# Feed-forward sums in two halves of a bank, products of 512 columns, and a new order of the mixers' steps

## The chip, the cores and the metric

The kernel runs on one core of one Trainium2 chip, with the engines TensorE (PE in the profile; its weight loads are PEld), VectorE (DVE), ScalarE (ACT), GpSimd (POOL) and SyncE (SP). The metric is the device time of one execution in microseconds (us), the median of several runs.

## What is computed

A trunk of two layers over 256 tokens of width 1024. Each layer is

```
x += 1/2 * SwiGLU(RMSNorm(x))               # ffn1: (silu(h @ w1) * (h @ w3)) @ w2, inner width 2816
h  = RMSNorm(x);  proj = h @ w_in           # width 3840: A retention, B HGRN2, C RG-LRU
x += concat(A, B, C) @ w_out                # A, B: 4 heads, chunks of 64 tokens; C: width 256
x += CrossAttn(RMSNorm(x), RMSNorm(mem))    # wq, wkv, wo; 4 heads of 256, 256 memory tokens
x += 1/2 * SwiGLU(RMSNorm(x))               # ffn2
```

and a final RMSNorm follows. All is float32; the weights of both layers, some 214 MB, are read once.

## The kernel before

The residual lies feature-major in SBUF (`xT`, 8 tiles of 128 features x 256 tokens). A float32 product on TensorE is made of float32r products: each operand is split into two parts, hi (rounded to float32r) and lo (the rest), and `mm3` (lines 175 to 179) issues hi·hi, hi·lo and lo·hi into one sum. Every product has a weight load of its own, of 128 columns, also where two that follow each other have the same weights.

The weights are packed on the host in pieces of 512 rows x 256 columns, in their order of use, and SP loads one piece (0.5 MB) with each DMA into one of four buffers `w_raw`. `_split` makes the parts: ScalarE copies to `w_hi` (line 82), VectorE subtracts to `w_lo` (line 83), three buffers each. `take`, called before a piece's products, issues loads five and splits three pieces ahead, at a priority over all else.

In `gemm_w` the weights are stationary and the activations move, 256 tokens wide: for a piece, two column tiles m, four k tiles and three products each. The feed-forward's first half uses it for w1 and w3, whose sums share a PSUM bank (the halves `[:, 0]` and `[:, 1]`, one bank per m); then VectorE multiplies the bank by the norm's `R` (line 372), ScalarE takes the silu, VectorE the product (line 376), and `split` gives the parts of g. Its second half, w2, sums 22 k tiles into one half of a bank; `add_tile` adds it to `xT` (line 345), and ScalarE and VectorE make the next norm's parts `xn_hi` and `xn_lo` (lines 257, 258).

In `gemm_x` the activations are stationary and the weights move, 256 columns wide, for two token tiles: the token-major columns of w_in, the memory's values and the last w2, which ends in the final norm (`final`).

The mixers are written as a list of steps, `STEPS`: a number is a column of w_in whose 256 columns are projected there; `decayN` are VectorE's and ScalarE's factors for HGRN2's head N (rows `E` and `qe`), `headN` its scores and values on TensorE, first token tile, then second; `rope`, `lru`, `retN`, `silu`, `ret`, `hgrn` and `lrutail` are the other branches and their outputs, `keys` the memory's keys. Then follow the values, w_out and the attention. A scheduler orders each engine's instructions within the priorities; work that is independent (keys, values) is drawn forward to fill TensorE.

A norm ends in `finish`: two products of one column per token tile (line 329; float32 products are issued as two each), a root on GpSimd, and one product of 256 columns in float32 (line 337), from which ScalarE copies `R` (line 338).

Of the kernel before, what the change touches and what calls it, by code (L numbers as in the profile page):

```python
# [26 lines left out]
SPLIT_AHEAD = 3  # L27
LOAD_AHEAD = 5
RAW_BUFS = 4
SPLIT_OFF = 100000  # L30
EVAC_OFF = 400
O_AHEAD = 1
KV_OFF = 100000
PART_BUFS = 3
E_BUFS = 1
# [15 lines left out]
SILU = "silu_and_others"  # silu, tanh, sin  # L51
# [4 lines left out]
class Weights:  # L56
    """Streams the packed pieces of the weights and splits them into two float32r parts."""

    def __init__(self, tc, pool, flat, pieces):
        self.tc, self.nc, self.pool = tc, tc.nc, pool  # L60
        self.flat, self.pieces = flat, pieces
        self.raw, self.parts = {}, {}
        self.n_load = self.n_split = self.n_take = self.off = 0

    def _load(self):
        i = self.n_load
        self.n_load += 1
        n = self.pieces[i].nk * CW
        t = self.pool.tile([P, 4 * CW], F32, name="w_raw", tag="w_raw", bufs=RAW_BUFS)
        self.nc.sync.dma_start(  # L70
            out=t[:, 0:n], in_=self.flat[self.off:self.off + P * n].rearrange("(p c) -> p c", p=P))
        self.off += P * n
        self.raw[i] = t.rearrange("p (k c) -> p k c", k=4)

    def _split(self):
        nc, i = self.nc, self.n_split
        self.n_split += 1
        nk = self.pieces[i].nk
        t = self.raw.pop(i)
        hi = self.pool.tile([P, 4, CW], F32R, name="w_hi", tag="w_hi", bufs=PART_BUFS)  # L80
        lo = self.pool.tile([P, 4, CW], F32R, name="w_lo", tag="w_lo", bufs=PART_BUFS)
        nc.scalar.copy(hi[:, 0:nk, :], t[:, 0:nk, :])  # L82
        nc.vector.tensor_tensor(  # L83
            out=lo[:, 0:nk, :], in0=t[:, 0:nk, :], in1=hi[:, 0:nk, :].bitcast(F32), op=ALU.subtract
        )
        self.parts[i] = (hi, lo)

    def take(self, key):
        i = self.n_take
        self.n_take += 1  # L90
        assert self.pieces[i].key == key, (self.pieces[i], key)
        with self.tc.high_priority(offset=SPLIT_OFF):
            while self.n_load < min(i + LOAD_AHEAD, len(self.pieces)):
                self._load()
            while self.n_split < min(i + SPLIT_AHEAD, len(self.pieces)):
                self._split()
        return (*self.parts.pop(i), self.pieces[i].nk)
# [5 lines left out]
IN_COLS = [1536, 1792, 2048, 2304] + [int(x) for x in STEPS if x.isdigit()]  # L103


# (column piece, first row tile) of xattn_wo: the first heads' rows of some columns fill the wait for the last heads
O_ORDER = [(c, 0) for c in range(O_AHEAD)] + [(c, 4) for c in range(O_AHEAD)]
O_ORDER += [(c, k0) for c in range(O_AHEAD, 4) for k0 in (0, 4)]

Piece = namedtuple("Piece", "key name l k0 nk c0")  # L110


def weight_pieces():
    """[nk * 128, 256] pieces of the weights in the order in which they are used"""
    out = []

    def gemm(key, name, l, nk, cs):
        for c in cs:
            for k0 in range(0, nk, 4):
                out.append(Piece(key, name, l, k0, min(4, nk - k0), c))  # L120

    for l in range(DEPTH):
        for f in ("ffn1", "ffn2"):
            if f == "ffn2":
                gemm("in", "w_in", l, KD, IN_COLS)
                gemm("kv", "xattn_wkv", l, KD, range(0, 2 * D, CW))
                gemm("out", "w_out", l, KD, range(0, D, CW))
                gemm("q", "xattn_wq", l, KD, range(0, D, CW))
                out += [Piece("o", "xattn_wo", l, k0, 4, c * CW) for c, k0 in O_ORDER]
            for c in range(0, FF, CW):  # L130
                gemm("w1", f + "_w1", l, KD, [c])
                gemm("w3", f + "_w3", l, KD, [c])
            gemm("w2", f + "_w2", l, KF, range(0, D, CW))
    # the first column's pieces in halves, for an early start
    return [out[0]._replace(nk=2, k0=k0) for k0 in range(0, KD, 2)] + out[2:]
# [9 lines left out]
def trunk(ctx: ExitStack, tc: tile.TileContext, a: dict, out: bass.AP, stop=None, dbg=None):  # L145
# [9 lines left out]
    class Bank:  # L155
        """A PSUM bank in which several sums may be open: only the first product clears the written bits"""
# [18 lines left out]
        def mm3(self, acc, lhs, rhs, begin, stop):  # L175
            (lh, ll), (rh, rl) = lhs, rhs
            self.mm(acc, lh, rh, begin, False)
            self.mm(acc, lh, rl, False, False)
            self.mm(acc, ll, rh, False, stop)

    class Act:
        """Activations that need a table: each table is loaded once for a run of them, in the order of the program"""
# [14 lines left out]
        def hold(self, i):  # L197
            """the next table waits for this instruction too"""
# [14 lines left out]
    W = Weights(tc, wp, a["weights"], weight_pieces())  # L213
# [37 lines left out]
    def split(hi, lo, src, scale=None):  # L251
        """hi + lo == src (* a column) with both parts in float32r"""
# [9 lines left out]
    def gemm_w(key, nk, x, accs):  # L262
        """acc += w[:, m]^T x for two column tiles m; accs = (bank, acc), x = (hi, lo) of [P, nk, S]"""
        xh, xl = x
        k0 = 0
        while k0 < nk:
            wh, wl, n = W.take(key)
            for m, (bank, acc) in enumerate(accs):
                for k in range(n):
                    sl = slice(m * P, (m + 1) * P)  # L270
                    bank.mm3(acc, (wh[:, k, sl], wl[:, k, sl]), (xh[:, k0 + k, :], xl[:, k0 + k, :]),
                             k0 + k == 0, k0 + k == nk - 1)
            k0 += n
            yield

    def gemm_x(key, nk, x, accs, begin=True):
        """accs[t] = (bank, acc), acc += x[:, t]^T w for two token tiles t"""
        xh, xl = x
        k0 = 0
        while k0 < nk:  # L280
            wh, wl, n = W.take(key)
            for t, (bank, acc) in enumerate(accs):
                for k in range(n):
                    sl = slice(t * P, (t + 1) * P)
                    bank.mm3(acc, (xh[:, k0 + k, sl], xl[:, k0 + k, sl]), (wh[:, k, :], wl[:, k, :]),
                             begin and k0 + k == 0, k0 + k == nk - 1)
            k0 += n
            yield
# [5 lines left out]
    class Norm:  # L294
        """RMSNorm of the residual: x * g goes out in two float32r parts, the 1 / rms is applied after the product"""

        def __init__(self, l, name, mem=False):
            self.gains = col(l, name)
            if not mem:
                self.hi = keep.tile([P, KD, S], F32R, name="xn_hi", tag="xn_hi", bufs=1)  # L300
                self.lo = keep.tile([P, KD, S], F32R, name="xn_lo", tag="xn_lo", bufs=1)
            self.ssq = small.tile([P, S], F32, name="ssq", tag="ssq", bufs=2)

        def parts(self, j, xj):
            split(self.hi[:, j, :], self.lo[:, j, :], xj, self.gains[:, j:j + 1])
# [777 lines left out]
```

## Time and profile before

| | us |
|---|---|
| median of 3 runs (lowest, highest) | 1275.28 (1275.21, 1276.19) |
| span of the profiled execution | 1272.7 |
| TensorE products, weight loads busy | 1256.4, 1249.8 |
| VectorE, ScalarE, GpSimd busy | 877.4, 682.3, 42.6 |

The profiled execution's own time is its span, 1272.7 us from the first to the last instruction; the median of the runs lies 2.6 us above it. A product's row lasts some 280 ns, since the rows of products overlap; how far the products stand apart is read from the chain of waits, which counts for each product the time until the next. The stretches: 6 to 204 us the first feed-forward (its second half from 140), to 387 the mixers with w_out, to 447 the attention, to 637 the second feed-forward; then the same for the second layer, with the last w2 from 1201 to 1265.

### The profile page before, as it was taken

To read this page: it belongs to the slowest core of one execution; us is meant where nothing else is said; L and a number is where in the kernel's file an instruction comes from. 1 tells how busy PE (TensorE), PEld (TensorE's weight loads), DVE (VectorE), ACT (ScalarE), POOL (GpSimd) and SP (SyncE) were. 2 spreads that over 40 slices of the span, in tenths; PEclk is the share of its full clock that TensorE was granted. 3 is DMA by queue.
4 is the path that set the end of the run, shared out by engine and by line. 5 is a ranking of instruction groups with operands and counts; after the bars stand their busy time and mean duration, and the time that the engine had idled before them with its cause. 6 is when DMAs were issued, how large, how long until landed. Compare 5 with 4: busy or idle time off the path is not lost.

```text
span 1272.7 us, 26847 instructions
## 1 busy us (share of the span) xinstructions
PE 1256.4 (99%) x11134; PEld 1249.8 (98%) x11134; DVE 877.4 (69%) x1456; ACT 682.3 (54%) x1149; POOL 42.6 (3%) x68
## 2 busy tenths in 40 slices
PE   7999999999999999999999999999999999999997
PEld 7999999999999999999999999999999999999997
DVE  7886656988776676665586665578877767666653
ACT  4554445656765654444464444465577656444543
POOL 5000000000100000000000000000001000000000
PEclk9999999999999999999999999999999999999999
DMA  8756566555465465665566665654545645666563
GB/s 269 211 175 184 174 185 190 157 149 150 117 182 165 115 184 183 183 182 182 183 209 202 181 184 179 187 177 154 159 121 149 183 133 165 183 183 182 168 181 100
DMA packets 61946, 219.64 MB, mean 173 GB/s; under 512 B 6912, under 2 KB 7168, under 8 KB 61568
## 3 DMA queue, kind: packets, MB, share of 16 engines
q1 hardware_dynamic: 60768, 213.55, 56.2%
q0 software_dynamic: 768, 3.86, 0.8%
q8 instruction: 87, 1.43, 0.5%
q10 hardware_dynamic: 288, 0.52, 0.1%
q14 instruction: 35, 0.29, 0.1%
HBM read 216.85 MB, written 1.05 MB: 171 GB/s over the span
## 4 chain that ended last, share of the span: by engine, by line
PE 83%; issue 15%; DVE 1%; DMA 0%; ACT 0%; POOLq 0%; POOL 0%; SPq 0%; ACTq 0%
PE mm L171 75%; PE aux L171 2%; PE aux L663 1%; PE mm L169 1%; PE aux L661 0%; PE aux L169 0%; DVE xn_lo L258 0%; PE aux L656 0%; PE aux L800 0%; PE aux L731 0%; PE aux L788 0%; DMA xT<-in_x_t_dram 0%; PE aux L337 0%; PE aux L901 0%; DVE w_lo L83 0%
## 5 line engine op out<-in xcount | busy, mean ns | idle before, releaser
L83 DVE TENSOR_TENSOR w_lo<-w_raw,w_hi 128x1024 fp32r<-128x1024 f32 (+1 forms) x414 | 498.9, 1206 | 281.3 <-ACT w_hi L82 278.6
L82 ACT CAST w_hi<-w_raw 128x1024 fp32r<-128x1024 f32 (+1 forms) x414 | 425.5, 1029 | 491.8 <-PE mm L171 371.3
L171 PE MATMUL mm<-xn_hi,w_lo 128*128 128x256 f32 x1728 | 487.6, 285 | 2.1 <-DVE w_lo L83 2.1
L171 PE MATMUL mm<-xn_lo,w_hi 128*128 128x256 f32 x1728 | 488.0, 284 | 0.0
L171 PE MATMUL mm<-xn_hi,w_hi 128*128 128x256 f32 x1620 | 457.8, 284 | 6.2 <-ACT w_hi L82 6.2
L171 PEld LDWEIGHTS mm<-xn_hi,w_lo 128*128 128x128 f32 x1728 | 330.4, 192 | 3.4 <-DVE w_lo L83 3.0
L171 PEld LDWEIGHTS mm<-xn_lo,w_hi 128*128 128x128 f32 x1728 | 331.6, 192 | 0.1
L171 PEld LDWEIGHTS mm<-xn_hi,w_hi 128*128 128x128 f32 x1620 | 311.1, 192 | 6.3 <-ACT w_hi L82 6.2
L171 PE MATMUL mm<-g_hi,w_hi 128*128 128x256 f32 x528 | 147.1, 280 | 0.0
L171 PE MATMUL mm<-g_lo,w_hi 128*128 128x256 f32 x528 | 146.1, 278 | 0.0
L171 PE MATMUL mm<-g_hi,w_lo 128*128 128x256 f32 x528 | 145.2, 281 | 0.0
L171 PEld LDWEIGHTS mm<-g_lo,w_hi 128*128 128x128 f32 x528 | 99.3, 188 | 0.0
L171 PEld LDWEIGHTS mm<-g_hi,w_hi 128*128 128x128 f32 x528 | 99.3, 188 | 0.0
L171 PEld LDWEIGHTS mm<-g_hi,w_lo 128*128 128x128 f32 x528 | 97.9, 188 | 0.0
L171 PE MATMUL mm<-w_hi,xn_lo 128*128 128x256 f32 x288 | 81.8, 284 | 0.0
L171 PE MATMUL mm<-w_lo,xn_hi 128*128 128x256 f32 x288 | 81.8, 284 | 0.0
L171 PE MATMUL mm<-w_hi,xn_hi 128*128 128x256 f32 x270 | 76.4, 285 | 0.0
L372 DVE TENSOR_TENSOR f_t<-mm,R 128x512 f32<-128x512 f32 x88 | 60.1, 687 | 3.6 <-ACT R L338 1.4
L171 PEld LDWEIGHTS mm<-w_hi,xn_lo 128*128 128x128 f32 x288 | 55.2, 192 | 0.1
L171 PEld LDWEIGHTS mm<-w_lo,xn_hi 128*128 128x128 f32 x288 | 55.2, 192 | 0.1
L171 PEld LDWEIGHTS mm<-w_hi,xn_hi 128*128 128x128 f32 x270 | 51.5, 192 | 0.0
L171 PE MATMUL mm<-w_lo,g_hi 128*128 128x256 f32 x176 | 49.3, 281 | 0.0
(269 smaller groups left out, 1955.7 us busy)
## 6 DMA issues: line engine op xcount, KB each, us to landing
w_raw<-in_weights_dram SPq DMA_DIRECT2D x394, 512.0 KB, 3.7
w_raw<-in_weights_dram SPq DMA_DIRECT2D x20, 256.0 KB, 2.7
m_t<-in_mem_t_dram POOLq DMA_DIRECT2D x2, 1024.0 KB, 7.9
xT<-in_x_t_dram SPq DMA_DIRECT2D x4, 256.0 KB, 4.9
cst<-in_c_cst_dram POOLq DMA_DIRECT2D x1, 696.0 KB, 6.4
gw<-in_gates_w_dram POOLq DMA_DIRECT2D x2, 256.0 KB, 8.5
fg<-in_final_norm_g_dram POOLq DMA_DIRECT2D x1, 512.0 KB, 5.9
out_dram<-y SPq DMA_DIRECT2D x2, 256.0 KB, 2.6
```

Source lines behind the costliest of these rows:

```text
L82: nc.scalar.copy(hi[:, 0:nk, :], t[:, 0:nk, :])
L83: nc.vector.tensor_tensor(out=lo[:, 0:nk, :], in0=t[:, 0:nk, :], in1=hi[:, 0:nk, :].bitcast(F32), op=ALU.subtract)
L169: nc.tensor.matmul(acc, lhsT, rhs, start=False, stop=stop, skip_group_check=True)
L171: i = nc.tensor.matmul(acc, lhsT, rhs, start=begin, stop=stop, skip_group_check=True)
L372: nc.vector.tensor_tensor(out=t, in0=uv[m].ap, in1=nrm.R[:, None, :].to_broadcast([P, 2, S]), op=ALU.mult)
L663: nc.tensor.matmul(sb[bs, i, :], ke[:, 1 + i, cb], qe[:, 1 + i, cb], start=True, stop=True, skip_group_check=True)
```

## The change

Hi and lo parts of an activation become one tile (`x[:, k, 0]` and `x[:, k, 1]`, side by side). Where the weights are stationary in a feed-forward, `mm_w` moves both through `w_hi` in one product of 512 columns, into both halves of a bank, and hi through `w_lo` in one of 256 into the second half; the two halves are added afterwards: in the first half by a ScalarE copy and a VectorE addition, before the multiplication by `R`, in w2 by a second addition in `add_tile`. w1 and w3 now have two banks each. w_in's feature-major columns, keys, w_out, wq and wo stay as three products of 256 (`mm3n`).

Where the activations are stationary, two column pieces that lie side by side are moved as 512 columns (`beside`), in the columns 0, 512, 1024 and 2560 of w_in, the values and the last w2; the order within `mm3` is new. Raw weights come in units of two pieces, in two buffers of 1 MB. The mixers' steps have a new order, both token tiles of a head are scored before their values, retention's heads are interleaved, and w_out opens four banks and starts with the k tiles 4 to 7.

```diff
-SPLIT_AHEAD = 3
-LOAD_AHEAD = 5
-RAW_BUFS = 4
+RAW_BUFS = 2
+SPLIT_AHEAD = PART_BUFS
@@ Weights._split
+        if unit.beside:
+            hi, lo = (t.rearrange("p (h k c) -> p h k c", h=2, k=2)[:, :, 0:nk, :] for t in (hi, lo))
+            t = self.raw[u].rearrange("p h (k c) -> p h k c", k=4)[:, :, at:at + nk, :]
+        nc.scalar.copy(hi, t)
+        nc.vector.tensor_tensor(out=lo, in0=t, in1=hi.bitcast(F32), op=ALU.subtract)
@@
-STEPS = ("2560 decay0 2816 head0 decay1 3328 3584 head1 decay2 0 256 head2 decay3 512 768 rope 1024 lru head3 ret0 ret1 "
-         "1280 3072 ret2 ret3 silu ret hgrn lrutail keys").split()
+STEPS = ("2560 decay0 3328 head0 decay1 3584 3072 head1 decay2 lru 0 head2 decay3 512 head3 "
+         "rope 1024 silu hgrn ret lrutail retout keys").split()
+W_COLS, X_COLS = (3328, 3584), (0, 512, 1024, 2560)
@@ Bank
         def mm3(self, acc, lhs, rhs, begin, stop):
             (lh, ll), (rh, rl) = lhs, rhs
             self.mm(acc, lh, rh, begin, False)
-            self.mm(acc, lh, rl, False, False)
-            self.mm(acc, ll, rh, False, stop)
+            self.mm(acc, ll, rh, False, False)
+            self.mm(acc, lh, rl, False, stop)
+
+        def mm_w(self, wh, wl, x, begin, stop):
+            self.mm(self.ap, wh, x, begin, stop)
+            self.mm(self.ap[:, 1, :], wl, x[:, 0, :], False, stop)
@@
+    def gemm_w(key, nk, x, banks):
+        k0 = 0
+        while k0 < nk:
+            wh, wl, n = W.take(key)
+            for m, bank in enumerate(banks):
+                for k in range(n):
+                    sl = slice(m * P, (m + 1) * P)
+                    bank.mm_w(wh[:, k, sl], wl[:, k, sl], x[:, k0 + k], k0 + k == 0, k0 + k == nk - 1)
+            k0 += n
+            yield
+
+    def gemm_x(key, nk, x, banks):
+        k0 = 0
+        while k0 < nk:
+            wh, wl, n = W.take(key)
+            for t, bank in enumerate(banks):
+                for k in range(n):
+                    sl = slice(t * P, (t + 1) * P)
+                    bank.mm3(bank.ap, (x[:, k0 + k, 0, sl], x[:, k0 + k, 1, sl]), (wh[:, :, k, :], wl[:, :, k, :]),
+                             k0 + k == 0, k0 + k == nk - 1)
+            k0 += n
+            yield
@@
-    def add_tile(j, acc, scale, nxt):
-        nc.vector.scalar_tensor_tensor(out=xT[:, j, :], in0=acc, scalar=scale, in1=xT[:, j, :],
-                                       op0=ALU.mult, op1=ALU.add)
+    def add_tile(j, halves, scale, nxt):
+        for h in halves:
+            nc.vector.scalar_tensor_tensor(out=xT[:, j, :], in0=h, scalar=scale, in1=xT[:, j, :],
+                                           op0=ALU.mult, op1=ALU.add)
@@ ffn
-                uv = [mm_bank(2) for _ in range(2)]
+                t = [fp.tile([P, 2, S], F32, name="f_t", bufs=3) for _ in range(2)]
                 for u, key in enumerate(("w1", "w3")):
-                    run(gemm_w(key, KD, nrm.x, [(b, b[:, u, :]) for b in uv]))
+                    banks = [mm_bank(2) for _ in range(2)]
+                    run(gemm_w(key, KD, nrm.x, banks))
+                    for m in range(2):
+                        p = fp.tile([P, S], F32, name="f_p", bufs=3)
+                        nc.scalar.copy(p, banks[m][:, 1, :])
+                        nc.vector.tensor_tensor(out=t[m][:, u, :], in0=banks[m][:, 0, :], in1=p, op=ALU.add)
@@ final
-        for c in range(4):
+        for c in range(2):
             banks = [mm_bank(2) for _ in range(2)]
-            run(gemm_x("w2", KF, g, [(b, b[:, 0, :]) for b in banks]))
-            cs = slice(c * CW, (c + 1) * CW)
+            run(gemm_x("w2", KF, g, banks))
+            cs = slice(c * 512, (c + 1) * 512)
@@ mixer
         def hgrn_head(h):
-            hgrn(h, 0)
-            hgrn(h, 1)
+            scs = [hgrn_scores(h, t) for t in range(2)]
+            ss = [hgrn_mask(scs[t], t) for t in range(2)]
+            for t in range(2):
+                hgrn_values(h, t, *ss[t])
```

On TensorE, within a column pair of the feed-forward's first half, one k tile before (a row is line, operation, tile <- moving, stationary operand, partitions x columns of the result; numbers tell buffers apart):

```order
L171 MATMUL mm_492<-xn_hi_113,w_hi_402 128x256
L171 MATMUL mm_492<-xn_lo_114,w_hi_402 128x256
L171 MATMUL mm_492<-xn_hi_113,w_lo_403 128x256
L171 MATMUL mm_492<-xn_hi_113,w_hi_402 128x256
L171 MATMUL mm_492<-xn_lo_114,w_hi_402 128x256
L171 MATMUL mm_492<-xn_hi_113,w_lo_403 128x256
```

and now, where the first bank's last products meet the second bank's first:

```order
L206 MATMUL mm_447<-xn_110,w_hi_389 128x512
L206 MATMUL mm_447<-xn_110,w_lo_390 128x256
L206 MATMUL mm_448<-xn_110,w_hi_369 128x512
L206 MATMUL mm_448<-xn_110,w_lo_370 128x256
L206 MATMUL mm_448<-xn_110,w_hi_369 128x512
```

Two products stand where three stood, one of them twice as wide.

On VectorE, a column pair of the feed-forward's first half before (`f_t` is the bank times R, `f_s` the silu's product, `g_lo` the lo part of g):

```order
L83 TENSOR_TENSOR w_lo_1112<-w_raw_1027,w_hi_1111 128x1024
L376 TENSOR_TENSOR f_s_1066<-f_s_1066,f_t_1064 128x256
L83 TENSOR_TENSOR w_lo_1142<-w_raw_1079,w_hi_1141 128x1024
L255 TENSOR_TENSOR g_lo_186<-f_s_1059,g_hi_185 128x256
L255 TENSOR_TENSOR g_lo_186<-f_s_1066,g_hi_185 128x256
L83 TENSOR_TENSOR w_lo_1172<-w_raw_1109,w_hi_1171 128x1024
L372 TENSOR_TENSOR f_t_1199<-mm_1077,R_167 128x512
L372 TENSOR_TENSOR f_t_1206<-mm_1078,R_167 128x512
```

and now (`f_p` is ScalarE's copy of a bank's second half; the rows of line 425 are the additions):

```order
L98 TENSOR_TENSOR w_lo_1273<-w_raw_1198,w_hi_1272 128x1024
L425 TENSOR_TENSOR f_t_1194<-mm_1247,f_p_1292 128x256
L427 TENSOR_TENSOR f_t_1194<-f_t_1194,R_168 128x512
L98 TENSOR_TENSOR w_lo_1324<-w_raw_1249,w_hi_1323 128x1024
L425 TENSOR_TENSOR f_t_1195<-mm_1248,f_p_1295 128x256
L431 TENSOR_TENSOR f_s_1299<-f_s_1299,f_t_1194 128x256
L427 TENSOR_TENSOR f_t_1195<-f_t_1195,R_168 128x512
L98 TENSOR_TENSOR w_lo_1344<-w_raw_1249,w_hi_1343 128x1024
L301 TENSOR_TENSOR g_180<-f_s_1299,g_180 128x256
```

Up to three operations now stand between two splits, where one or two stood.

On TensorE in the first layer's mixers, around the first score product of HGRN2's fourth head (`half` and its number; `mem` are products of the keys, `hi,hs` the values of a head) before:

```order
L171 MATMUL mm<-mem_l,w_hi 128x256
L171 MATMUL mm<-mem_h,w_lo 128x256
L169 MATMUL mm<-mem_h,w_hi 128x256
L656 MATMUL aux<-half_2_109 128x128
L171 MATMUL mm<-mem_l,w_hi 128x256
```

and now:

```order
L206 MATMUL mm<-w_hi,xn 128x512 x4
L206 MATMUL aux<-hi,hs 128x96
L720 MATMUL aux<-half_2_106 128x128
L206 MATMUL mm<-mem_n,w_hi 128x256 x2
L206 MATMUL aux<-hi,hs 128x96
L720 MATMUL aux<-half_3_108 128x128
L206 MATMUL mm<-w_lo,xn 128x512
L206 MATMUL mm<-w_hi,xn 128x512 x2
```

The head, which stood among the keys, behind w_in's last token-major columns, now stands amid products of w_in (`w_hi,xn`), with both token tiles together.

## Rows read from the trace of the kernel before

**Rows 1.** The page: span; busy us (share) x instructions of each engine.
```profile
span 1272.7 us, 26847 instructions
PE 1256.4 (99%) x11134; PEld 1249.8 (98%) x11134; DVE 877.4 (69%) x1456; ACT 682.3 (54%) x1149; POOL 42.6 (3%) x68
```
**Rows 2.** Waits: engine, line <- waited for: total us, times, longest.
```profile
DVE w_lo L83 <- ACT w_hi L82: 278.6, 271, 2.6
...
PE mm L171 <- ACT w_hi L82: 6.2, 1, 6.2
...
PE mm L171 <- DVE w_lo L83: 2.1, 3, 1.0
```
**Rows 3.** Chain of waits in order of time: start us, us, what, products.
```profile
31.20 9.96 PE mm L171 x83
...
135.74 67.83 PE mm L171 x575
```
**Rows 4.** Chain of waits, 205 to 214 us: a norm's end.
```profile
208.85 0.34 PE aux L329 x4
...
213.25 0.43 PE aux L337 x2
```
**Rows 5.** Timeline of the loads, 212.8 to 213.8 us: start us, us, what.
```profile
212.97 0.31 PEld L337 LDWEIGHTS aux<-r_diag,mean 128*128 128x128 f32 x2
213.30 0.19 PEld L171 LDWEIGHTS mm<-xn_hi,w_lo 128*128 128x128 f32 x1
213.52 0.19 PEld L171 LDWEIGHTS mm<-xn_hi,w_hi 128*128 128x128 f32 x1
```
**Rows 6.** Groups of products: out<-in, shapes xcount | busy us, mean ns | idle before.
```profile
L171 PE MATMUL mm<-xn_lo,w_hi 128*128 128x256 f32 x1728 | 488.0, 284 | 0.0
...
L171 PE MATMUL mm<-g_lo,w_hi 128*128 128x256 f32 x528 | 146.1, 278 | 0.0
...
L171 PE MATMUL mm<-w_hi,xn_lo 128*128 128x256 f32 x288 | 81.8, 284 | 0.0
...
L171 PE MATMUL mm<-w_lo,g_hi 128*128 128x256 f32 x176 | 49.3, 281 | 0.0
...
L171 PE MATMUL mm<-w_hi,mem_l 128*128 128x256 f32 x128 | 36.6, 286 | 0.0
```
**Rows 7.** Groups of VectorE and ScalarE, same columns.
```profile
L83 DVE TENSOR_TENSOR w_lo<-w_raw,w_hi 128x1024 fp32r<-128x1024 f32 x394 | 483.2, 1227 | 263.1 <-ACT w_hi L82 260.4
...
L372 DVE TENSOR_TENSOR f_t<-mm,R 128x512 f32<-128x512 f32 x88 | 60.1, 687 | 3.6 <-ACT R L338 1.4 <-PE mm L171 0.5
...
L376 DVE TENSOR_TENSOR f_s<-f_s,f_t 128x256 f32<-128x256 f32 x88 | 33.8, 419 | 0.1
...
L345 DVE SCALAR_TENSOR_TENSOR xT<-mm,xT 128x256 f32<-128x256 f32 x56 | 23.0, 420 | 19.3 <-PE mm L171 19.2
...
L338 ACT COPY R<-aux 128x256 f32<-128x256 f32 x8 | 3.0, 371 | 6.7 <-PE aux L337 6.7
```
**Rows 8.** Stretches: us, then busy (x) of PE, PEld, DVE, ACT, POOL; clock, DMA, GB/s.
```profile
6.00:143.70 137.70, 135.42 (x1102) 134.30 (x1103) 104.65 (x163) 72.80 (x119) 16.82 (x19) 1.00 0.68 206
...
460.00:580.20 120.20, 120.20 (x1003) 120.15 (x1002) 79.45 (x106) 57.81 (x87) 0.00 (x0) 1.00 0.61 181
...
648.00:770.00 122.00, 122.00 (x1019) 121.95 (x1018) 85.70 (x123) 61.28 (x95) 0.00 (x0) 1.00 0.64 193
```
**Rows 9.** Stretches of the first mixers, same columns.
```profile
204.00:310.00 106.00, 106.00 (x1135) 104.88 (x1134) 89.34 (x204) 62.05 (x111) 3.66 (x8) 1.00 0.54 160
...
220.00:240.00 20.00, 20.00 (x211) 19.83 (x210) 18.81 (x47) 14.83 (x24) 0.56 (x1) 1.00 0.53 157
240.00:260.00 20.00, 20.00 (x212) 19.84 (x211) 18.49 (x47) 9.16 (x19) 0.76 (x2) 1.00 0.53 154
```
**Rows 10.** The page: DMA issues, xcount, KB each, us to landing.
```profile
w_raw<-in_weights_dram SPq DMA_DIRECT2D x394, 512.0 KB, 3.7
```

More of the change, by code (lines that the diff above doesn't have):

```diff
@@ L77, in _split @@
         self.n_split += 1
[L78 to L85, printed above, removed]
+        u, unit, at, nk = self.steps[i]
+        while self.n_load < len(self.pieces) and self.pieces[self.n_load][0] <= u:
+            self._load()
+        hi = self.pool.tile([P, 4 * CW], F32R, name="w_hi", tag="w_hi", bufs=PART_BUFS)
+        lo = self.pool.tile([P, 4 * CW], F32R, name="w_lo", tag="w_lo", bufs=PART_BUFS)
+        if unit.beside:
+            hi, lo = (t.rearrange("p (h k c) -> p h k c", h=2, k=2)[:, :, 0:nk, :] for t in (hi, lo))
+            t = self.raw[u].rearrange("p h (k c) -> p h k c", k=4)[:, :, at:at + nk, :]
+        else:
+            hi, lo = (t.rearrange("p (k c) -> p k c", k=4)[:, 0:nk, :] for t in (hi, lo))
+            t = self.raw[u].rearrange("p h (k c) -> p h k c", k=4)[:, at, 0:nk, :]
+        nc.scalar.copy(hi, t)
+        nc.vector.tensor_tensor(out=lo, in0=t, in1=hi.bitcast(F32), op=ALU.subtract)
         self.parts[i] = (hi, lo)
@@ L326, in finish @@
             pr = aux_bank()
-            self.R = small.tile([P, S], F32, name="R", tag="R", bufs=2) if R is None else R
             for t in range(2):
@@ L331, in finish @@
             rsqrt_col(self.rc, pr[:, 0:2], 2)
+            self.R = small.tile([P, S], F32, name="R", tag="R", bufs=2) if R is None else R
             dg = small.tile([P, 2, P], F32, name="r_diag", tag="r_diag", bufs=1)
@@ L380, in ffn @@
             run(setup or ())
-            if not last:
-                run(residual("w2", KF, (gh, gl), 0.5, nxt))
-            else:
-                final((gh, gl), fp)
+            if last:
+                return final(g, fp)
+            for c in range(0, KD, 2):
+                banks = [mm_bank(2) for _ in range(2)]
+                run(gemm_w("w2", KF, g, banks))
+                for m in range(2):
+                    add_tile(c + m, [banks[m][:, u, :] for u in range(2)], 0.5, nxt)
+            nxt.finish()
     def final(g, fp):
@@ L564, in mixer @@
         for j in (0, 2):
-            run(w_pair(hq, j))
+            w_pair(hq, j)
             v = hq[:, j:j + 2, :]
@@ L858, in mixer @@
                 x_cols(int(step))
-        v_mem = [values(h) for h in range(NH)]
-        run(residual("out", KD, (mh, ml), 1.0, nxt))
+        v_mem = values() + values()
+        for c in range(0, KD, 4):
+            banks = [mm_bank(2) for _ in range(4)]
+            for k0 in (4, 0):
+                for i in range(0, 4, 2):
+                    wh, wl, n = W.take("out")
+                    for m in range(2):
+                        for k in range(n):
+                            sl, bank = slice(m * P, (m + 1) * P), banks[i + m]
+                            bank.mm3n(bank[:, 0, :], (wh[:, k, sl], wl[:, k, sl]),
+                                      (mix[:, k0 + k, 0, :], mix[:, k0 + k, 1, :]), k0 + k == 4, k0 + k == 3)
+            for m in range(4):
+                add_tile(c + m, [banks[m][:, 0, :]], 1.0, nxt)
+        nxt.finish()
         return k_mem, v_mem
```

276 lines of the change are left out of this document (148 added, 128 removed).

## The prediction

> **What bounds the kernel now.** I read the page's table of busy times first [rows 1]: TensorE is busy for 1256.4 of 1272.7 us, its weight loads for 1249.8, VectorE for 877.4 and ScalarE for 682.3. A busy TensorE says little by itself, since its products overlap, so I then asked whom it waited for: by the table of waits, 8.3 us in all, for two parts of weights at the start [rows 2]. Nothing feeds TensorE too late; the time of the kernel is the sum of its products' spacings, and a change is worth what it takes off that sum.
>
> The spacing is in the chain of waits, where products that follow each other without a wait are merged. In the feed-forward's first half 83 products of 256 columns take 9.96 us, 120.0 ns each; in its second half 575 take 67.83 us, 118.0 ns each [rows 3]. What sets these 120 ns? Two pairs of unlike products tell it [rows 4]. Four products of one column each, every one behind its own load of 128 columns of weights, take 0.34 us, and the step from a load to the next is about 113 ns (the first of the four is already loaded: 0.34 / 3). So a load costs some 113 ns even where the product is nothing. And the two products of line 337, in float32 and 256 columns wide, stand 215 ns apart (0.43 / 2), although one of them, too, has its load between. There the product's own stream is the longer, and the load vanishes beneath it. The timeline of the loads shows the same [rows 5]: the two loads of line 337 are 0.12 us apart (0.31 less one load's 0.19), each starts when the product before it starts, then comes one after 0.33 and the next after 0.22 us, the length of the long stream. So every spacing is the longer of two: the load of the next weights, 118 to 120 ns beside a running product, and the product's own stream. A product of 256 columns is too short to cover the load that follows it.
>
> **The change, part by part.** (1) *Feed-forward with the weights stationary.* Three products of 256 columns (hi·hi, hi·lo, lo·hi) become one of 512 and one of 256. The 512 columns are not in the trace. Lower bound: 215 ns, the pair of line 337, if a float32r column takes half the time of a float32 column there. Upper bound: 240 ns, twice the 120 of today, if the stream and not the load makes the 120. I take 218, near the lower: the rows show a load of 120 gone wholly beneath a long stream, but beside float32r streams loads are 5 to 7 ns longer than the 113 of the one-column products, and part of such friction may come to lie on the stream. The 256 that follows still pays for a load, 120 (118 in the second half). First half: 4 feed-forwards x 11 column pairs x 2 matrices x 8 x 2 = 1408 triples (the other 320 of the 1728 in [rows 6] belong to other projections, which stay as three). 3 x 120 - (218 + 120) = 22 ns, 1408 x 22 = 31.0 us. Second half, three feed-forwards: the 528 triples of [rows 6], 354 - (218 + 118) = 18 ns, 9.5 us.
>
> (2) *Token-major products of 512 columns.* Two products of 256 become one of 512, all three kinds. Of the 288 x 3 with xn stationary, the four column pairs of w_in make 768; the memory's values make 128 x 3 = 384; the last product 176 x 3 = 528 [rows 6]. 576 pairs x (240 - 218) = 12.7 us, 264 pairs x (236 - 218) = 4.8 us. Sum of (1) and (2): 58.0 us.
>
> The skill speaks against this sum in one place. The Trainium skill ("TensorE: Matmul & The Clock Gate", section Back-to-back issue gap) gives the gap of a lone stream as its columns over the clock and 2.5 ns, so 109 ns for 256 columns and 216 for 512, by which 2776 products fewer would be worth 2776 x 2.5 = 7 us, as an estimate. The trace does not agree, since 256 columns stand 118 to 120 ns apart here and one column 113; I give it no chance of its own. In Part 3 of the same page of the Trainium skill (packing small matmuls, The mechanism) a load overlaps a running product only in other row groups; by that, a load would come on top of every 512 columns. The trace contradicts it with the 215 ns of line 337, which hold a stream and a load.
>
> (3) *What the other engines get.* Each column pair of the first half now sums in two halves of a bank: 4 copies on ScalarE out of PSUM (0.37 each, the row of R) and 4 additions on VectorE (0.42, the row of xT) are added, 44 per feed-forward; the multiplication by R stays at 0.69, its operand now in SBUF [rows 7]. In the first feed-forward VectorE has 104.7 us of work in 137.7 us [rows 8]; with 44 x 0.42 = 18.5 it has 123.1, while the stretch shrinks by 352 x 22 ns = 7.7 to 130.0: 95%. In the second it is 79.5 + 18.5 = 98.0 of 112.5, 87%; in the third 85.7 + 18.5 = 104.2 of 114.3, 91%. ScalarE in the second: 57.8 + 16.3 of 112.5, 66%. The cover is three split steps ahead, some 2 x 2.7 us of TensorE's work between the moment when a buffer comes free and the moment when it must be full, and by the order at most three operations (1.5 us) stand between two w_lo. So I charge 3 us for the first feed-forward and 1 for the other three (bounds 0 and 10). Behind a w_lo that is late stands TensorE itself, and nothing else.
>
> (4) *Small ends.* The first product now wants the lo part of xn as well, one more operation of VectorE (0.5 us), and the first 12 us are bound by loading and splitting, so their saving of 0.7 us is not had: 1.2 us. At the very end each addition, square and gain is 512 wide instead of 256, 0.27 us longer each on the path (0.69 against 0.42): 0.8 us. The second addition per tile in the second half adds 0.42 us to the tail of three feed-forwards; the next stage's products on the six earlier tiles cover it: nothing (1.3 us without the cover).
>
> (5) *The mixers' order.* The products that are moved cost the same. What can be lost is cover: the fourth head's scores now stand ahead of the last w_in column instead of behind it and rope, so VectorE's four decays must be done earlier, while TensorE's w_in work is shorter. VectorE is the engine that is close: 89.3 of 106.0 us over the first mixers and 18.5 to 18.8 of 20 in the stretches of the decays [rows 9]; its work there stays, and TensorE's work in the same stretch shrinks by 192 x 22 ns = 4.2 us. I charge 2 us a layer, 4 (bounds: nothing, as now, where TensorE waits for no head; and 12 us, if the stretch becomes VectorE's). The raw weights' buffers, now two of 1 MB instead of four of half, leave a load a whole unit of time (5.4 us) for the 3.7 us that it takes by the page's table of issues [rows 10]: nothing.
>
> Sum: -58.0 + 4.0 + 1.2 + 0.8 + 4.0 = -48.0. The profiled execution's span of 1272.7 us stands 2.6 under the median of the runs (1275.28), which lies around the span and stays; 1275.3 - 48.0 = **1227 us**.
>
> **The rivals.**
> *A cost per product.* The 120 ns could be 107 of stream (half of line 337's 215) and 13 that every product pays, load or not. Then 512 columns cost 226, and the change saves 13.3 ns on 1408 + 576 and 11.3 on 528 + 264: 35.3 us; with the 10 us of (3) to (5), 1250. For it: the spacing is nearly constant. Against: 215 ns for line 337, which leaves at most 2 ns over twice 107.
> *VectorE sets the pace of the first halves.* A column pair has 4 w_lo (1.23), 4 additions, 2 x 0.69 and 4 x 0.42: 9.7 us, against 11.5 of TensorE now (96 x 0.120) and 10.8 after (32 x 0.338). If 0.47 us per w_lo of its wait for w_hi (278.6 us in all now, [rows 2]) can't be filled with other work, the first halves gain nothing: 1275.3 - 27.0 + 6 = 1254. For it: a strict order on the engine. Against: that wait is one of an engine that is ahead.
> *The mixers lose their cover*: 12 us a layer instead of 2, 1247. For it, the 18.8 of 20 us; against, TensorE waits for no head now, though VectorE is as full in those stretches [rows 2, 9].
> *The other side: the stream sets the 120.* If TensorE can't take in a float32r column faster than 120 / 256 ns, 512 columns cost 240, no product gets cheaper, and (3) to (5) remain: 1285. It decides from 235 ns per 512 columns (218 + 48.0 / 2.776). For it: the spacing of 256 columns is never far below 113 to 120. Against: the 113 of the one-column products, which have no stream.
>
> **How the numbers follow.** Forecast 0.64; a cost per product 0.14; VectorE 0.09; the mixers 0.05; the stream 0.08. A measurement of this kernel can tell about 0.2% (2.6 us) from no change. The forecast's own range is 1209 (215 ns, no new stalls) to 1240. The first three rivals end under 1272 nearly always: faster 0.89, within 0.2% 0.03, slower 0.08. The range reaches to the cost per product and to VectorE's case and leaves out the stream: 1208 to 1258.
>
> **What would show it.** In the profile after: runs of 512-column products about 218 ns apart and pairs of 512 and 256 about 338; busy weight loads well under the span, since there are 2776 fewer; w_lo's waits for w_hi shrunk; TensorE's waits under 15 us, most of them in the first feed-forward for w_lo. 226 or 240 ns there make it one of two rivals; gaps of TensorE behind w_lo in the first halves, or behind hs and E in the mixers, the other two. It is wrong if the sum of spacings has fallen and the span has not.

## The result, and the profile after

The changed kernel takes 1252.72 us (median of four runs, 1251.94 to 1253.19) against 1275.39 (1275.21 to 1276.19): ratio 0.982, interval 0.9806 to 0.9834. It is faster by 22.7 us, inside the range, but less than half of the 48.0 that I forecast; the time is that of the rival "a cost per product" (1250).

The head of the page, as in [rows 1]:

```profile
span 1250.1 us, 21651 instructions
...
PE 1230.2 (98%) x8358; PEld 1102.1 (88%) x8358; DVE 938.3 (75%) x1645; ACT 733.9 (59%) x1303; POOL 43.4 (3%) x68
```

TensorE is busy to nearly the same share (98 against 99%) with 2776 products fewer, and its loads have fallen below the span by 148 us. It waits 11.4 us for others, 3 more than before; in the table of waits, which answers to [rows 2] (total us, times, longest):

```profile
PE mm L206 <- DVE xn L304: 7.1, 1, 7.1
PE mm L206 <- DVE w_lo L98: 3.4, 6, 1.1
PE mm L206 <- ACT o L300: 0.9, 2, 0.4
```

So the time is still the sum of the products' spacings. The chain of waits merges the feed-forward's products now as it did in [rows 3] (start us, us, what, products):

```profile
30.73 25.50 PE mm L206 x145
```

175.9 ns a product, every other one 512 columns wide: 352 a pair, where I forecast 338 and three products took 360. How the pair splits is in the timeline of TensorE in the second feed-forward, where the starts (first column, us) count and the durations overlap:

```profile
499.67 0.40 PE L206 MATMUL mm<-xn,w_hi 128*128 128x512 f32 x1
499.90 0.28 PE L206 MATMUL mm<-xn,w_lo 128*128 128x256 f32 x1
500.02 0.40 PE L206 MATMUL mm<-xn,w_hi 128*128 128x512 f32 x1
500.25 0.28 PE L206 MATMUL mm<-xn,w_lo 128*128 128x256 f32 x1
500.37 0.40 PE L206 MATMUL mm<-xn,w_hi 128*128 128x512 f32 x1
```

Some 230 ns behind each wide product, 120 behind each narrow one. The stretches of the changed kernel, with the columns of [rows 8] (the first feed-forward's first half; the second's; its second half, with g; the third's first half; then the two that answer to [rows 9]):

```profile
7.00:137.00 130.00, 127.98 (x714) 110.24 (x715) 114.04 (x200) 82.47 (x156) 15.57 (x19) 1.00 0.57 209
460.00:560.00 100.00, 100.00 (x568) 86.72 (x567) 78.56 (x125) 59.04 (x108) 0.00 (x0) 1.00 0.51 190
570.00:627.00 57.00, 57.00 (x329) 50.11 (x328) 34.09 (x49) 26.83 (x38) 0.00 (x0) 1.00 0.53 189
655.00:752.00 97.00, 96.75 (x557) 84.56 (x558) 79.86 (x129) 57.82 (x106) 0.00 (x0) 1.00 0.54 196
...
204.00:310.00 106.00, 104.91 (x1030) 95.25 (x1030) 90.11 (x206) 64.96 (x110) 3.47 (x8) 1.00 0.42 153
222.00:242.00 20.00, 20.00 (x180) 17.77 (x179) 17.89 (x43) 12.32 (x16) 0.00 (x0) 1.00 0.52 188
```

The clock is granted in full in all of them, and in the second to fourth TensorE is busy all but without a break while VectorE has 18 to 40% of its time left. With xn a pair takes 2 x 100 / 568 = 352 ns, with g 2 x 57 / 329 = 347. The additions cost VectorE and ScalarE what I had taken from [rows 7]; in the changed kernel's groups, same columns:

```profile
L424 ACT COPY f_p<-mm 128x256 f32<-128x256 f32 x176 | 64.2, 366 | 37.0 <-PE mm L206 35.3
L425 DVE TENSOR_TENSOR f_t<-mm,f_p 128x256 f32<-128x256 f32 x176 | 73.0, 417 | 0.1
```

### The profile page after: what moved, and what is told of

The parts are those of the page before. It is cut to its first block, busy times and chain, and to the rows that moved or that the text cites. A ratio compares the mean times of both kernels' runs of the same rounds, so it can differ in the third digit from the quotient of the medians.

```text
span 1250.1 us, 21651 instructions
## 1 busy us (share of the span) xinstructions
PE 1230.2 (98%) x8358; PEld 1102.1 (88%) x8358; DVE 938.3 (75%) x1645; ACT 733.9 (59%) x1303; POOL 43.4 (3%) x68
## 4 chain that ended last, share of the span: by engine, by line
PE 81%; issue 15%; DVE 3%; ACT 1%; DMA 0%; POOLq 0%; POOL 0%; SPq 0%; DVEq 0%; ACTq 0%
PE mm L206 74%; PE aux L206 2%; PE aux L727 1%; DVE w_lo L98 1%; PE aux L725 0%; ACT w_hi L97 0%; DMA xT<-in_x_t_dram 0%; DVE xn L304 0%; PE aux L204 0%; PE aux L720 0%; PE aux L877 0%; PE aux L806 0%; PE aux L998 0%; PE aux L863 0%; PE aux L399 0%
## 5 line engine op out<-in xcount | busy, mean ns | idle before, releaser
L206 PE MATMUL mm<-xn,w_hi 128*128 128x512 f32 (+1 forms) x2028 | 608.4, 362 | 7.1 <-DVE xn L304 7.1
L206 PE MATMUL mm<-xn,w_lo 128*128 128x256 f32 x1728 | 480.2, 282 | 2.3 <-DVE w_lo L98 2.3
L206 PEld LDWEIGHTS mm<-xn,w_hi 128*128 128x128 f32 x2028 | 360.4, 189 | 66.2 <-ACT w_hi L97 7.1
L206 PEld LDWEIGHTS mm<-xn,w_lo 128*128 128x128 f32 x1728 | 327.5, 190 | 8.7 <-DVE w_lo L98 5.3
L206 PE MATMUL mm<-g,w_hi 128*128 128x512 f32 x528 | 181.7, 392 | 0.0
L206 PE MATMUL mm<-g,w_lo 128*128 128x256 f32 x528 | 143.1, 281 | 0.0
L206 PEld LDWEIGHTS mm<-g,w_hi 128*128 128x128 f32 x528 | 96.8, 188 | 19.5
L206 PEld LDWEIGHTS mm<-g,w_lo 128*128 128x128 f32 x528 | 99.4, 188 | 2.6
L206 PE MATMUL mm<-w_hi,xn 128*128 128x512 f32 (+1 forms) x318 | 89.1, 374 | 0.0
L424 ACT COPY f_p<-mm 128x256 f32<-128x256 f32 x176 | 64.2, 366 | 37.0 <-PE mm L206 35.3
L425 DVE TENSOR_TENSOR f_t<-mm,f_p 128x256 f32<-128x256 f32 x176 | 73.0, 417 | 0.1
L404 DVE SCALAR_TENSOR_TENSOR xT<-mm,xT 128x256 f32<-128x256 f32 x80 | 32.5, 419 | 22.6 <-PE mm L206 22.6
```

Of the source, the lines that this page charges most:

```text
L206: i = nc.tensor.matmul(acc, lhsT, rhs, start=begin, stop=stop, skip_group_check=True)
L404: nc.vector.scalar_tensor_tensor(out=xT[:, j, :], in0=h, scalar=scale, in1=xT[:, j, :], op0=ALU.mult, op1=ALU.add)
L424: nc.scalar.copy(p, banks[m][:, 1, :])
L425: nc.vector.tensor_tensor(out=t[m][:, u, :], in0=banks[m][:, 0, :], in1=p, op=ALU.add)
```

## The experiments

**1. Products alone.** A kernel of nothing but products, 32 of a kind behind each other in one bank, eight loads in turn, then other places, other types, fewer stationary columns, and stretches beside VectorE, ScalarE and DMAs. In short:

```
for n in (512, 448, 384, 320, 256, 192, 128, ...):
    segment([(big[:, X0:X0 + n], big[:, (i % 8) * 128:(i % 8) * 128 + 128]) for i in range(32)])
...
```

> Products alone, 32 of a kind behind each other, with no other engine at work but in the last four stretches; the kernel's own computation is left out. In the changed kernel 512 float32r columns stand 226 to 241 ns apart where I had counted 218. Theory A, a cost per product that does not shrink with the width: (columns / 2.4 GHz) + 13 ns as long as a load of 113 ns is the shorter, so 512 -> 226, 448 -> 200, 384 -> 173, 320 -> 147, 256 -> 113 to 120, and 113 from 192 columns down; a stationary operand of 64 columns changes 512 by 0 to 7 ns. Theory B, a stream slower than one column per cycle: 512 / 448 / 384 / 320 / 256 in proportion, 240 / 210 / 180 / 150 / 120 or 226 / 198 / 170 / 141 / 113. Theory C, other engines take away reads: alone 512 -> 215 and 256 -> 113, beside VectorE's, ScalarE's or the DMAs' work 226 to 240 and 120. Theory D, addresses: the pitch of one width differs by 7 to 20 ns with the place of the moving operand.

Its chain of waits; a name gives the columns (w) and, where they are not 128, the stationary columns (m); bf is bfloat16, f float32 (each of its 32 products is issued as two, so 64 are counted):

```profile
38.90 7.25 PE x512w L208 x32
46.15 6.49 PE x448w L208 x32
52.64 5.57 PE x384w L208 x32
58.21 4.69 PE x320w L208 x32
62.90 3.84 PE x256w L208 x32
66.73 3.55 PE x192w L208 x32
70.28 3.55 PE x128w L208 x32
...
94.78 7.36 PE x512m64w L208 x32
...
113.27 3.63 PE x256m64w L208 x32
...
286.07 6.92 PE x512bf L208 x32
292.99 3.49 PE x256bf L208 x32
296.49 13.81 PE x256f L208 x64
```

Divided by the count: 227, 203, 174, 147 and 120 ns for 512 to 256 columns, that is the columns at 2.4 GHz (the clock is granted in full there) and 13 to 16 ns, whatever the width; 111 for 192 columns and for 128, a floor that I take for the load. That is theory A. Theory B falls, since 512 and 256 columns are not in proportion. The extra belongs to float32r: bfloat16 takes 216 and 109, and the two halves of a float32 product of 256 columns 216 each.

The stationary operand has a part in it, though. With 64 stationary columns instead of 128, 256 columns took 113 ns instead of 120, and 512 took 230 instead of 227. Every product here had a load of its own, so the runs do not tell what a product would pay without one.

The Trainium skill ("TensorE: Matmul & The Clock Gate", section Back-to-back issue gap) gives for the gap of an isolated product at the full clock its columns over 2.4 GHz and 2.5 ns; the bfloat16 rows agree with it, and no row in float32r does.

Theory C falls too; stretches of this kernel with TensorE alone, beside VectorE, and beside VectorE and ScalarE:

```profile
318.00:329.00 11.00, 11.00 (x63) 9.71 (x64) 0.91 (x7) 0.00 (x0) 0.00 (x0) 1.00 0.00 0
330.00:341.00 11.00, 11.00 (x64) 9.73 (x64) 10.21 (x14) 0.00 (x0) 0.00 (x0) 1.00 0.01 1
342.00:353.00 11.00, 11.00 (x64) 9.60 (x62) 10.79 (x14) 9.70 (x10) 0.00 (x0) 1.00 0.00 0
```

As many products in 11 us, whether the others rest or work. Beside DMAs, with their engines 86% busy, 256 columns took the same 120 ns, and 512 took 227 as soon as the clock was granted in full (427 before that, at half the clock). Of theory D there was a trace: with the moving operand 64 bytes further 512 columns took 233 and 256 took 118.

**2. Three products of 256 again in the feed-forwards**, without the copies and additions of the halves, all else as changed:

```
-                    bank.mm_w(wh[:, k, sl], wl[:, k, sl], x[:, k0 + k], ...)
+                    bank.mm3n(acc, (wh[:, k, sl], wl[:, k, sl]), (x[:, k0 + k, 0, :], x[:, k0 + k, 1, :]), ...)
```

> The changed kernel with the feed-forwards' products as three of 256 columns again, in both halves (the additions and copies of the halves go too); token-major products and the mixers' order stay as changed. From the traces' spacings (a triple 360 against 351 ns, 1408 times, and 354 against 348.4, 528 times) I expect 12.7 + 3.0 = 16 us more than the changed kernel, 1268. The prediction's size of 22 and 18 ns would make it 40 us more, 1293. If the additions on VectorE cost what I charged (6 us), 10 us more, 1262.

1267.69 us (1267.47 to 1268.60), ratio to before 0.9943 (0.9926 to 0.9959). The feed-forwards' part of the change brings 15.0 us of the 22.7. By their spacings the products alone bring 17.1 (the table below), so the copies, the additions and the waits that they make cost some 2 us at most. The 7.7 that are left belong to all the rest together, the token-major products (7.5 by their spacings) and the new order.

**3. The heads in an order close to the old one.**

```
-STEPS = ("2560 decay0 3328 head0 decay1 3584 3072 head1 decay2 lru 0 head2 decay3 512 head3 "
-         "rope 1024 silu hgrn ret lrutail retout keys").split()
+STEPS = ("2560 decay0 3072 head0 decay1 3328 3584 head1 decay2 0 head2 decay3 512 "
+         "rope 1024 lru head3 ret silu hgrn lrutail retout keys").split()
```

> The changed kernel with the mixers' steps in an order close to the old one: the fourth head behind rope, the last w_in column and the LRU's gates. From the stages' lengths the mixers gained 0.9 and 2.6 us where their products' spacings fell by 3.0 each, so some 2.5 us were lost in both layers. If the new order is what loses them, this kernel is 2.5 us faster, 1250; if the wider products lose them whatever the order, it is within 1 us of the changed kernel, 1252 to 1253; if the new order hides more than it loses, it is slower, 1255.

1250.52 us (1250.18 to 1251.44), ratio 0.9808 (0.9793 to 0.9822): 2.2 us faster than the changed kernel, about what a measurement can tell, and what the stages' lengths said. TensorE's waits for w_lo fall from 3.4 to 1.3 us. The new order costs some 2 us where I charged 4.

**4. Where the operands lie.** Products alone at other places within 512 bytes (s: the moving operand shifted by so many bytes), and 512 and 256 in turn (pair):

```
segment([(big[:, X0 + d:X0 + d + n], big[:, (i % 8) * 128:(i % 8) * 128 + 128]) for i in range(32)])
```

> Products alone again, 32 of a kind; the kernel's own computation is left out. With moving and stationary operand at the same place within 512 bytes, 512 columns took 226.7 ns and 256 took 120.0, but 512 and 256 in turn 352.9 for both, 6 more than their sum; with the moving operand 64 bytes further 233.3 and 117.8. Theory: the relative place within 512 bytes sets which few ns come on top, so a scan gives 226 to 234, 113 to 120 and 346 to 353 for the pair, with shifts of 32 bytes at 233 / 117 / 347 as g shows in the changed kernel, the same for a shift of the stationary operand the other way, and no change when both are shifted. Rival: the extra belongs to the change of width, and no shift moves the pair by more than 2 ns. In groups of four wide and four narrow products: 4 x 226.7 + 4 x 120 + one or two changes, 346.7 to 349 a pair.

Its chain of waits:

```profile
39.16 7.25 PE x512s0b L208 x32
46.42 3.83 PE x256s0b L208 x32
50.25 5.65 PE xpairs0b L208 x32
...
100.72 5.55 PE xpairs32b L208 x32
...
240.85 7.46 PE x512s448b L208 x32
248.32 3.63 PE x256s448b L208 x32
...
408.85 5.62 PE xgroup4g L208 x32
```

The place does move the spacing: 256 columns from 120 to 113 ns at 448 bytes, while 512 columns go the other way, 227 to 233; a pair 353 at one place and 347 at 32 bytes. It is not the place alone: at 64 bytes 512 columns took 229 here (7.33 us for the 32) and 233 in experiment 1 (7.47), behind other products. Both operands shifted alike changed nothing (5.65 us for the pairs, 3.83 for 256 columns). At no place does a pair come near 338. I first took the groups of four for 342 ns a pair, from a mean that counted fewer wide than narrow products; the row says 5.62 / 16 = 351.

**5. xn 32 bytes further.**

```
+                x = keep.tile([P, KD * 2 * S + 128], F32R, name="xn", tag="xn", bufs=1)
+                self.x = x[:, 8:8 + KD * 2 * S].rearrange("p (k u s) -> p k u s", k=KD, u=2)
```

> The changed kernel with xn 32 bytes further within its 512, nothing else. In the changed kernel a pair of 512 and 256 takes 353.3 ns with xn (which lies as the weights do within 512 bytes) and 346.7 with g (32 bytes further). If the place is the reason: 1408 x 6.7 = 9.4 us less in the first halves, 960 products of 256 at 117 to 118 instead of 120, 2 us less, and 384 products with xn stationary at 233 instead of 226.7, 2.5 us more: 1252.7 - 9 = 1244. If the place isn't the reason, but the matrix (number of steps, the order of the loads), it stays within 1 us of 1252.7.

1247.69 us (1247.25 to 1248.50), ratio 0.9785 (0.9769 to 0.9801): 5.0 us faster than the changed kernel by the place alone. Its second feed-forward has 578 products in 100 us instead of 568:

```profile
460.00:560.00 100.00, 100.00 (x578) 88.61 (x577) 80.33 (x129) 59.61 (x108) 0.00 (x0) 1.00 0.52 191
```

That is 346 a pair, as forecast for that stretch; the whole is less than the 9 us that I expected, since the changed kernel's pairs do not stand at 353 everywhere (349.4 in the mean of the four feed-forwards).

**6. Groups of a width, alone and in the kernel.**

```
-                    bank.mm_w(wh[:, k, sl], wl[:, k, sl], x[:, k0 + k], ...)
+                    bank.mm(bank.ap, wh[:, k, sl], x[:, k0 + k], ...)
+                for k in range(n):
+                    bank.mm(bank.ap[:, 1, :], wl[:, k, sl], x[:, k0 + k, 0, :], ...)
```

> Products alone, 64 of 512 and 256 columns in turn, in groups of 1, 2, 4 and 8 of a width, at five places; the kernel's own computation is left out. Alone in turn a pair took 353, in groups of four and eight 341.7 and 340.7. Theory: each change from the narrow product to the wide one costs some 12 ns beyond a product's own cost, so groups of 1 / 2 / 4 / 8 give 353 / 347 / 342 to 344 / 341 to 342 a pair at place 0, and less spread with the place. Rival: not the number of changes but the sequence of the weights' places does it, then groups of 2 already give 341, or those of 4 still 347 at other places. Three products of 256, as in the mixers: 120 each at place 0, 117 at 32 bytes, 113 to 118 at 448, grouped or not.

> The changed kernel with the feed-forwards' products in another order: for each bank and step of weights first its four products of 512 columns, then its four of 256. Nothing else is changed. If the 353.3 and 346.7 ns of a pair are a matter of the change of width, the pairs fall to 342: 1408 x 11.5 + 528 x 5 = 18.8 us less than the changed kernel, 1234. If the scheduler takes groups apart (it does in some places), two thirds of it, 1240. If in the kernel, with other engines at work and two banks in turn, the place decides and not the order, 1252.

> Groups of eight (both banks' wide products, then both banks' narrow ones) and the mixers' steps in the order of the second experiment. If both gains add up: 1252.7 - 19.5 - 2.2 = 1231. If groups of eight let the narrow products wait less for w_lo or more for a bank, the stalls show it, within 2 us of that.

Alone, 32 pairs in groups of one and of four at the same place, from the chain of waits:

```profile
38.49 11.29 PE xg1s0b L208 x64
...
60.95 11.23 PE xg4s0b L208 x64
```

353 and 351 ns a pair: at this place the changes of width cost next to nothing, and my premise was the miscount of experiment 4. In the kernel groups gain nothing: groups of four 1257.81 us (1256.80 to 1259.14; 0.986, 0.9844 to 0.9876), 5.1 more than the changed kernel, of which 2.8 are new waits of TensorE for f_t; groups of eight with the old heads 1252.07 (1251.73 to 1252.33; 0.9817, 0.9803 to 0.9832), 1.5 more than experiment 3 without groups. At 64 bytes the same kernel of products does gain by groups of two, 11.30 to 11.05 us or 353 to 345 ns a pair; no whole kernel was run that way.

**7. The kernel before with 64 unused bytes ahead of the weights' parts.** No instruction and no order changes, only addresses:

```
+        if self.pad is None:
+            self.pad = self.pool.tile([P, 16], F32, name="pad", tag="pad", bufs=1)
         hi = self.pool.tile([P, 4, CW], F32R, name="w_hi", tag="w_hi", bufs=PART_BUFS)
```

> The kernel before with 64 unused bytes ahead of the parts of the weights; every instruction and its order stay. Alone, 256 columns took 120.0 ns with moving and stationary operand at one place within 512 bytes, 117 to 118 at 32 or 64 bytes, 113.3 with the stationary operand 64 bytes further. Here xn and the memory move at one place with the weights now and would be at that last place: 5184 x 6.6 + 384 x 6.3 = 36.6 us less; token-major products 120 -> 117.8: 1248 x 2.1 = 2.6 less; g, the mix and o stay, 32 bytes off. Expected 1275.4 - 39 = 1236, which is faster than the changed kernel. If the place only counts where PE has no other engines beside it, 1275; if VectorE's splits become the bound at 340 a triple, 1250 or more.

1241.74 us (1241.11 to 1242.57), ratio 0.9735 (0.9722 to 0.9749): 33.8 us faster than before, and 11.0 faster than the changed kernel. The chain of waits of its first and second feed-forward, to be laid beside the 9.96 us for 83 products in [rows 3]:

```profile
99.23 9.78 PE mm L174 x83
...
480.02 9.41 PE mm L174 x83
```

117.8 ns in the first feed-forward and 113.4 in the second, where both took 120.0. Had the first run at 113.4 too, its 1056 products would have saved 4.6 us more, most of what is missing from the 1236 expected.

**8. The changed kernel with the same 64 bytes.** The edit is that of 7.

> The changed kernel with the same 64 bytes. Pairs of 512 and 256 took 353.4 at that place alone, 352.9 at the place they have: 0 to 4 us more for 1408 pairs; its 960 + 384 products of 256 columns 113.3 instead of 120: 8.9 less; token-major 512 columns 229 to 233 instead of 227 to 228.5: 1 to 3 more. Expected 1247 to 1250. Then at this place the change makes the kernel slower, 1249 against 1236; if the place isn't the reason for the small gain, both kernels move by the same.

1252.74 us (1252.20 to 1253.64), ratio 0.9822 (0.9808 to 0.9835): no change. In the means of the trace, without waits, narrow products gain (the memory's 119.7 to 116.3 ns) and wide ones lose (the feed-forward's 233.2 to 234.5, the token-major ones' with xn 228.5 to 230.5). At this place the change makes the kernel 11 us slower.

**9. All together**: experiment 2's products, experiment 3's order, 64 bytes ahead of the weights' parts and 416 ahead of g, the mix and o:

```
+    gap = ctx.enter_context(tc.tile_pool(name="gap", bufs=1))
+    nc.gpsimd.memset(gap.tile([P, 104], F32, name="gap"), 0.0)
```

> A version to beat both: the feed-forwards as three products of 256 (the first experiment), the old order of the heads (the second), 64 bytes ahead of the weights' parts and 416 ahead of g, the mix and o, so that these too stand 64 bytes behind the weights within 512. From 1267.7: heads -2.2; 5184 x 6.6 + 384 x 6.3 = -36.6; g 1584 x 4.5 = -7.1; mix and o 768 x 3.4 = -2.6; token-major 512 columns +1 to +3. Expected 1221. If three products at 113 outrun the splits, TensorE's waits for w_lo grow and it is 1225 to 1235.

1248.91 us (1248.00 to 1249.14), ratio 0.979 (0.9776 to 0.9803), far from 1221. It waits 2.0 us for w_lo, less than the changed kernel; its spacings are not those expected. The chain of waits, second feed-forward:

```profile
503.05 9.78 PE mm L211 x83
```

117.8 ns, where the kernel of experiment 7 has 113.4, at the same place within 512 bytes. What differs in these products is that lo lies beside hi (1 KB apart) and not behind all of it (8 KB).

**10. Which of the two spacings a stretch gets.** The feed-forward's triples alone, at the place of experiment 7, with lo 8 KB (apart8) or 1 KB (apart1) from hi, and ahead of each stretch one product of some odd width (o, in columns); "zero" is the place without the 64 bytes:

```
ps = [(big[:, x0:x0 + odd], w(w0))] if odd else []
ps += [(xh, wh), (xl, wh), (xh, wl)] for each k, 24 times
```

> Triples of 256 columns alone, as in the feed-forward, 72 of a kind; the kernel's own computation is left out. With the weights 64 bytes further the kernel before ran its first feed-forward at 117.8 ns a product and the next three at 113.3; three products with hi and lo side by side ran at 117.8 in all four. Theory 1, the layout decides (lo 8 KB behind hi against 1 KB): 113.3 for the first and 117.8 for the second, whatever product stands ahead. Theory 2, the rhythm in which the stretch begins decides, and then holds: with a first product of 0 to 416 columns both layouts show now the one, now the other. At the place without the 64 bytes 120.0 always.

Its chain of waits (72 products, 73 with the odd one):

```profile
39.35 8.17 PE apart8o0c L208 x72
47.52 8.16 PE apart1o0c L208 x72
55.68 8.59 PE apart8o32c L208 x73
64.27 8.59 PE apart1o32c L208 x73
72.86 8.29 PE apart8o96c L208 x73
81.15 8.59 PE apart1o96c L208 x73
...
174.44 8.64 PE zero8o0c L208 x72
```

Theory 2, in the main. At the same place and with the same layout a stretch runs at 113.3 or at 117.8 ns to its end, as the product ahead of it has it (113.3 behind five of eight entries with lo 8 KB away, behind three of eight with 1 KB, two entries telling the layouts apart); at the place without the 64 bytes it is 120.0 behind all four that were tried. So the layout alone does not explain experiment 9, whose cause stays open, and which rhythm a stretch of a whole kernel falls into I can't foretell. Experiment 7 has both in one kernel, at one place and with one layout.

## Why the prediction was wrong

| term (us) | forecast | measured |
|---|---|---|
| feed-forward, first halves: 1408 triples | -31.0 | 359.7 to 349.4 ns: -14.5 |
| second halves: 528 | -9.5 | 353.4 to 348.4: -2.6 |
| token-major, 576 pairs | -12.7 | 239.7 to 228.3: -6.6 |
| the last product, 264 pairs | -4.8 | 236.6 to 233.3: -0.9 |
| new waits (VectorE, the mixers) | +8.0 | +0.4 |
| start and end | +2.0 | +1.6 |
| sum | -48.0 | -22.6 |

The measured spacings are means of both traces without the waits (what exceeds 260 ns behind a wide product, 140 behind a narrow one, counts as one). Start and end are the first product's start and what follows the last one's; the spans differ by 22.6, and the row of the waits is what is left of that. It is a net: experiment 3 shows that the order alone costs 2 us.

*The step that failed* is the size of the 512-column product: "I take 218, near the lower". It measures 227 alone, and 228 to 233 in the means of the kernel's four groups. Behind it stands the sentence "every spacing is the longer of two: the load of the next weights [...] and the product's own stream". The first pair of rows that I had for it, the one-column products, does show the load: 113 there, 111 in experiment 1. But the spacing is not the longer of the two. It is 107 of stream and 13 on top for 256 columns, and the same 13 for 320 columns, whose 147 ns no load of 111 can have made, and for 512. Whether the 13 belong to the product or to its load beside the stream is not shown; the 113 ns with 64 stationary columns suggest that the load has a part in them. What is shown is that a wider stream does not hide them. The second pair, line 337's 215 ns, is right and was the wrong witness: it is float32, and experiment 1 shows 216 there, 2.5 over twice 107, where float32r pays 13. The nearest row was near in length only, not in the type.

*What could have told it.* In the same trace of before the mix's products stand 116.7 ns apart in the mean and xn's 120.0, with loads and streams of one shape. The chain of waits shows it in w_out (192 of these products are the mix's), 116.9 each:

```profile
364.47 24.32 PE mm L171 x208
```

Two numbers where a load of one shape would give one: I named "118 to 120 beside a running product" friction of the loads and left the 113 to 117 out.

*The rival* "a cost per product" (1250, 0.14) had the cost that does not shrink with the width, and 226 ns. My argument against it, that 215 ns leave at most 2 over twice 107, fell with the type. That its time came within 3 us is in part luck: its 35.3 us were too many, as the four terms show (24.6), since a pair at xn's place costs more than its two products alone, and the 10 us that it took over for waits and ends were too many by 8. "The stream sets the 120" is refuted by the 227 of experiment 1.

*The rest held.* VectorE's additions cost what the rows said and made next to nothing wait (TensorE 3.4 us for w_lo, 2.1 before); in the first feed-forward it has 88% of the stretch, not 95%. "VectorE sets the pace" and "the mixers lose their cover" did not come true, the latter but for 2 us. Start and end were right in size: the first product waits for xn's lo, 0.9 us later than before. TensorE's waits stayed under 15 us, but most of them are this one and not those for w_lo.

What stays open is why the place and the entry set 113, 118 or 120 ns. The runs show that the place does, alone and in whole kernels, that the entry does in products alone, and that the work of other engines changes neither the 120 nor the 227 of products alone.

## What to carry to other kernels

Take the price of an operation from a row of the same type, and where rows of one shape differ by a few per cent (117 and 120 ns here), ask why before building on either. Before rewriting a kernel that is bound by its products' spacing, move one operand by some tens of bytes: here 64 bytes gave 33.8 us, more than the rewrite's 22.7, and in the rewritten kernel nothing. Fewer and wider products saved only what each product pays on top of its stream, and part of that went to the wider ones' place.

## What the runs showed of the hardware

- A float32r product with a load of its own stands 13 to 16 ns over its columns at 2.4 GHz, from 256 to 512 columns at one place; a bfloat16 product, and each half of a float32 one over twice its columns, 2 to 3. Products of 192 and of 128 columns both take 111 ns.
- With 64 stationary columns instead of 128, 256 columns take 113 ns instead of 120, and 512 take 230 instead of 227.
- What a float32r product pays depends on where moving and stationary operand lie to each other within 512 bytes: 256 columns take 113 to 120 ns, 512 take 227 to 234, and the best place for 256 columns (448 bytes) is among the worst for 512.
- At one place two steady rhythms exist, 113.3 and 117.8 ns, and a stretch of products alone keeps the one that it began in.
- VectorE at 93 to 98% and ScalarE at 88% of a stretch beside it take nothing from TensorE's spacing.
